# Block 1's norms in columns of tokens, the mix output's second half tile by tile, and the FFN's first weights split earlier

## The chip, the cores and the metric

The kernel runs on one core of one Trainium2 chip. The metric is device time in microseconds (us) of one execution; the times are given as the median of several runs, and the trace is of one profiled execution.

## The reference

Two blocks work on x of 512 tokens by 1024 features, in fp32. Block 1 has two layers; each is a norm, a projection with attention, a short convolution and gates (unchanged here), a projection of the merged branches back to 1024 features (the *mix output*), a second norm and an MLP with relu squared. Block 2 is one layer with a modulated norm, a token mixer and a SwiGLU FFN.

```python
def rmsnorm(x, g):
    xf = x.astype(jnp.float32)
    y = xf * lax.rsqrt(jnp.mean(xf * xf, axis=-1, keepdims=True) + EPS)
    return (y * g.astype(jnp.float32)).astype(x.dtype)
...
    for l in range(DEPTH):
        u = rmsnorm(x, norm_mix[l])
        proj = u @ w_in[l]
...
        x = x + merged @ w_mix_out[l]
        u = rmsnorm(x, norm_mlp[l])
        x = x + jnp.square(jax.nn.relu(u @ w_mlp_up[l])) @ w_mlp_down[l]
    return rmsnorm(x, norm_final)
...
        x = x + gt_m[:, None, :] * y
        h = modulate(rms_norm(x, g_ffn[l]), sh_f, sc_f)
        x = x + gt_f[:, None, :] * swiglu(h, w_gate[l], w_up[l], w_down[l])
```

## The kernel before

**Layout.** x stays in the chip's memory as eight tiles x0 to x7 of 128 features by 512 tokens. A weight matrix is streamed from DRAM in loads of 512 KB (`raw`, a ring of 8). Each load is split into a high part (`wh`, a cast on ScalarE, L217) and a low part (`wl`, a subtraction on VectorE, L218), and the activations are split likewise (`hilo`, L455 and L456; `prep`, L463 and L464, which also scales by the norm's gain). An fp32 product is then three matmuls (L279, L280, L281): high by high, high by low, low by high. A matmul on 512 columns of tokens fills one PSUM bank; four `mm` banks take the four output tiles that are under way.

**Order.** The program is a list of items. A *unit* is one piece of weights: at each unit the program issues the loads up to 5 units ahead and the splits up to 2 units ahead. *do* items run in their place; *bg* items are taken up one by one, so many to a unit as *rate* says. Each engine then works through its own queue in order, and semaphores hold an instruction until what it needs is there. So a matmul that waits holds every matmul behind it.

**Norm.** `square` adds up the squares of x0 to x7 in a tile `ss` (L494 on ScalarE, L495 on VectorE). `rstd` sums `ss` over the 128 partitions by a matmul with a matrix of ones (L501), and everything after it works on 128x512, although all partitions hold the same: a square root (L503), L504, a reciprocal (L505) and three steps of refinement (L511 to L513). The products with the weights don't wait for it, since they run on x times gain; the result `rs` enters as the banks are emptied (L928 for the MLP's first products).

**Mix output to MLP.** `linear` computes the mix output in two halves of four tiles; a half takes k-tiles 0 to 3 on all four tiles first and then k-tiles 4 to 7, in loads of 4 k-tiles by 256 columns. So x4 to x7 are finished 12 matmuls apart, at the very end (L912 adds the bank to x). The MLP's first 512 columns (`u0`) are a plain `linear`, in four pieces on the four banks; the other columns go by `seven`, seven products of half size in place of eight (L401 to L403, 256 columns each), for which sums and differences of x tiles are made (`mix`, L476 to L479, on tiles that L980 has scaled). These sums for four pairs of tiles (xk, xk+4) are background work during `u0`. `up(c)` and `down(c-1)` are then meshed.

**Norms in columns.** Block 1's end and block 2 already have another form: `colsum` (L1045) puts tokens on partitions (a 128x1 matmul for each 128 tokens), the arithmetic is done on 128x2 or 128x4, and `spread` (L1054, L1056) brings it back to all partitions by a diagonal matrix times ones. After layer 2's last `down`, the final norm and block 2's first norm run this way on each half of the tokens, then `hnorm` (L1066, L1076, L1079) writes block 2's input. Block 2's FFN starts the same way, with `gateup` (L1533 to L1535) as its first products and `y` (L1612) as scaling.

## Time and profile before

| | before |
|---|---|
| median of 3 runs | 2082.54 us (2080.67 to 2082.63) |
| profiled execution | 2082.21 us, span 2079.9 us |
| TensorE (PE) busy | 2041.5 us, 98% of the span |
| VectorE (DVE) busy | 1575.5 us, 76% |
| ScalarE (ACT) busy | 982.9 us, 47% |
| mean granted TensorE clock | 0.991 of full speed |

The span is the time from the first to the last instruction of the trace; 2.3 us of the profiled execution lie outside it. A matmul counts as busy whatever its clock. In the chain of work that ended last, PE has 91%.

### The profile page before, as it was taken

Reading aid. Unit: us, or ns where it says so; the run is one execution under the profiler, and the core shown is the slowest. Engines: PE = TensorE matmul, PEld = TensorE weight load, DVE = VectorE, ACT = ScalarE, POOL = GpSimd, SP = SyncE. Lnnn points to the kernel's source line nnn. Section 1 sums busy time; section 2 is a strip of 40 time slices with the busy share of each in tenths; the row PEclk is TensorE's granted clock in tenths of the full one; section 3 lists DMA queues with packets and bytes.
Section 4 is the critical chain, followed back from the end, with each engine's and each line's share of the span. In section 5 each row is a group of like instructions: output and inputs, shape, how many; then the busy total and the mean of one; then the engine's idle time right before and its main releaser. Section 6 shows DMA issues by size and latency. Waiting matters only on the chain.

```text
span 2079.9 us, 29624 instructions
## 1 busy us (share of the span) xinstructions
PE 2041.5 (98%) x11552; PEld 1759.0 (85%) x11552; DVE 1575.5 (76%) x2801; ACT 982.9 (47%) x1699; POOL 19.5 (1%) x33
## 2 busy tenths in 40 slices
PE   9999999899999999999998999999999998999999
PEld 7888888799999878888886999998877787999998
DVE  6999666797877669977667888877777378777775
ACT  5324773544444432339545444445477744443442
POOL 0000000000000000000000000000000000000000
PEclk9999999999999999999998999999999999999999
DMA  7333212244444333331223444443321112233331
GB/s 233 96 97 101 72 62 92 91 142 142 145 160 142 102 97 92 101 102 53 78 84 104 144 148 152 153 132 91 92 72 62 51 61 82 92 102 104 100 100 42
DMA packets 199020, 216.60 MB, mean 104 GB/s; under 512 B 10721, under 2 KB 178017, under 8 KB 198881
## 3 DMA queue, kind: packets, MB, share of 16 engines
q1 hardware_dynamic: 198880, 214.73, 32.8%
q8 instruction: 90, 1.47, 0.3%
q14 instruction: 50, 0.40, 0.1%
HBM read 212.60 MB, written 2.10 MB: 103 GB/s over the span
## 4 chain that ended last, share of the span: by engine, by line
PE 91%; DVE 6%; ACT 2%; issue 1%; DMA 0%; POOL 0%; SPq 0%; DVEq 0%; ACTq 0%; POOLq 0%
PE mm L279 13%; PE mm L280 13%; PE mm L281 13%; PE mm L401 7%; PE mm L402 7%; PE mm L403 7%; PE at L279 7%; PE at L280 7%; PE at L281 7%; PE at L540 1%; PE ot L574 1%; PE mm L430 1%; PE mm L431 1%; PE mm L432 1%; PE at L559 1%
## 5 line engine op out<-in xcount | busy, mean ns | idle before, releaser
L217 ACT CAST wh<-raw 128x1024 fp32r<-128x1024 f32 (+3 forms) x272 | 277.5, 1024 | 537.0 <-PE mm L280 220.1
L279 PE MATMUL mm<-g,wh 128*128 128x512 f32 (+2 forms) x1328 | 506.9, 383 | 2.4 <-ACT g L1076 1.6
L281 PE MATMUL mm<-g,wl 128*128 128x512 f32 (+2 forms) x1328 | 503.4, 379 | 0.0
L280 PE MATMUL mm<-g,wh 128*128 128x512 f32 (+2 forms) x1328 | 502.4, 379 | 0.0
L218 DVE TENSOR_TENSOR wl<-raw,wh 128x1024 fp32r<-128x1024 f32 (+3 forms) x272 | 321.6, 1184 | 128.5 <-ACT wh L217 127.2
L401 PE MATMUL mm<-g,wh 128*128 128x256 f32 x1288 | 367.7, 285 | 14.9 <-DVE g L928 12.6
L402 PE MATMUL mm<-g,wh 128*128 128x256 f32 x1288 | 367.4, 285 | 1.0 <-DVE g L456 1.0
L403 PE MATMUL mm<-g,wl 128*128 128x256 f32 x1288 | 367.3, 285 | 0.0
L279 PEld LDWEIGHTS mm<-g,wh 128*128 128x128 f32 (+1 forms) x1328 | 250.1, 189 | 51.8 <-issue 4.3
L280 PEld LDWEIGHTS mm<-g,wh 128*128 128x128 f32 (+1 forms) x1328 | 250.1, 188 | 45.7 <-issue 1.2
L281 PEld LDWEIGHTS mm<-g,wl 128*128 128x128 f32 (+1 forms) x1328 | 250.0, 188 | 45.7
L401 PEld LDWEIGHTS mm<-g,wh 128*128 128x128 f32 x1288 | 250.1, 194 | 22.4 <-issue 8.9
L402 PEld LDWEIGHTS mm<-g,wh 128*128 128x128 f32 x1288 | 249.6, 194 | 7.0 <-DVE g L456 1.4
L403 PEld LDWEIGHTS mm<-g,wl 128*128 128x128 f32 x1288 | 249.6, 194 | 0.5
L279 PE MATMUL at<-g,g 128*128 128x512 f32 x608 | 239.7, 394 | 1.4 <-ACT g L455 1.4
L280 PE MATMUL at<-g,g 128*128 128x512 f32 x608 | 239.5, 394 | 0.1
L281 PE MATMUL at<-g,g 128*128 128x512 f32 x608 | 237.7, 391 | 0.0
L217 ACT CAST wh<-ws 128x1024 fp32r<-128x1024 f32 x69 | 72.4, 1050 | 216.0 <-PE mm L402 205.2
L281 PEld LDWEIGHTS at<-g,g 128*128 128x128 f32 x608 | 114.7, 189 | 24.8
L279 PEld LDWEIGHTS at<-g,g 128*128 128x128 f32 x608 | 115.2, 189 | 22.4 <-ACT g L455 3.0
L280 PEld LDWEIGHTS at<-g,g 128*128 128x128 f32 x608 | 115.2, 190 | 19.5 <-DVE g L456 0.9
L218 DVE TENSOR_TENSOR wl<-ws,wh 128x1024 fp32r<-128x1024 f32 x69 | 84.4, 1223 | 60.6 <-ACT wh L217 60.6
(265 smaller groups left out, 2716.7 us busy)
## 6 DMA issues: line engine op xcount, KB each, us to landing
raw<-w_in SPq DMA_DIRECT2D x111, 512.0 KB, 3.8
raw<-w_mlp_up SPq DMA_DIRECT2D x64, 512.0 KB, 3.8
raw<-w_mlp_down SPq DMA_DIRECT2D x64, 512.0 KB, 3.4
g<-w_ada SPq DMA_DIRECT2D x96, 256.0 KB, 4.2
raw<-w_gate SPq DMA_DIRECT2D x22, 512.0 KB, 3.6
raw<-w_up SPq DMA_DIRECT2D x22, 512.0 KB, 3.6
raw<-w_down SPq DMA_DIRECT2D x22, 512.0 KB, 3.4
raw<-w_mix_out SPq DMA_DIRECT2D x16, 512.0 KB, 3.4
```

What stands on the lines that cost most here:

```text
L217: act.copy(hi, raw)
L218: dve.tensor_sub(lo, raw, hi.bitcast(F32))
L279: pe.matmul(ps, wh, hi[:, cs], start=st, stop=False)
L280: pe.matmul(ps, wh, lo[:, cs], start=False, stop=False)
L281: S["pe"] = pe.matmul(ps, wl, hi[:, cs], start=False, stop=en)
L401: pe.matmul(ps, wh, hi, start=first and m == 0 and k == 0, stop=False, skip_group_check=True)
L402: pe.matmul(ps, wh, lo, start=False, stop=False, skip_group_check=True)
L403: S["pe"] = pe.matmul(ps, wl, hi, start=False, stop=k == 3, skip_group_check=True)
L430: pe.matmul(ps, xh, wh, start=kb + k == 0, stop=False)
L431: pe.matmul(ps, xl, wh, start=False, stop=False)
L432: pe.matmul(ps, xh, wl, start=False, stop=kb + k == KT - 1)
L540: pe.matmul(ps[:, :WM], qs[hh][:, i * P : (i + 1) * P], ks[hh][n][:, :WM], start=n == 0, stop=n == 1)
```

## The change

1. **Norms.** The four norms inside block 1 go from `rstd` to `rstd1` (`colsum` into four columns, then arithmetic on 128x4) and `rstd2` (`spread` to 128x512 and a copy by ScalarE). `norm2` no longer collects the tokens' column with four instructions, since `rstd1` leaves it.
2. **Mix output.** Its second half is computed tile by tile: four units of 8 k-tiles by 128 columns, so that x4 to x7 are finished 24 matmuls apart. The operand sums `mix(0)` to `mix(2)` are issued right after x4, x5 and x6; `mix(3)` stays in the background of `u0`.
3. **mesh** puts each piece of `down` one piece of `up` later.
4. **Layer 2's end.** The last `up` is meshed with only the first half of `down(6)`; then come the first half of `down(7)` and, on two halves of the tokens, the second half of `down(6)` and `down(7)` in one.
5. **ahead.** From the second half of block 2's output projection until `gateup(1, 1)`, splits run up to 5 and loads up to 8 units ahead.

```diff
@@ -86,6 +86,8 @@
                 bg.extend(pay)
             elif kind == "rate":
                 rate = pay
+            elif kind == "ahead":
+                self.ahead, self.early = pay
             elif kind == "drain":
                 while bg:
                     bg.popleft()()
@@ -113,8 +115,11 @@
     out = []
     for i, x in enumerate(a):
         out.extend(x)
-        for p in b[i * len(b) // n : (i + 1) * len(b) // n]:
-            out.extend(p)
+        if i:
+            for p in b[(i - 1) * len(b) // n : i * len(b) // n]:
+                out.extend(p)
+    for p in b[(n - 1) * len(b) // n :]:
+        out.extend(p)
     return out
@@ -234,7 +239,7 @@
             us.append({"src": (ch, 0, ch[2], c, min(uw, ch[4] - c)), "narrow": narrow})
         return us
-    def linear(W, row0, kts, c0, widths, xs, evac, parts_=1, narrow=False, newbank=mmbank):
+    def linear(W, row0, kts, c0, widths, xs, evac, parts_=1, narrow=False, newbank=mmbank, bytile=False):
@@ -248,6 +253,10 @@
         TW = T // parts_
         steps = []
         kbase = 0
+        if bytile:
+            ch = chunk(W, row0, total, c0, cw)
+            steps = [(0, total, [{"src": (ch, 0, total, c, P)}]) for c in range(0, cw, P)]
+            kts = []
         for kt in kts:
             ch = chunk(W, row0 + kbase * P, kt, c0, cw)
             us = halves(ch, narrow)
@@ -494,17 +503,21 @@
             act.activation(sq[:, cs], x[j][:, cs], AF.Square, scale=scale)
             dve.tensor_add(S[key, "ss"][:, cs], S[key, "ss"][:, cs], sq[:, cs])
-    def rstd(key):
-
-        ps = atbank()
-        with tc.issue_after(S["pe"].ins):
-            pe.matmul(ps, ones, S[key, "ss"], start=True, stop=True)
-        sd, v, rs = slot(), slot(), slot()
-        act.activation(sd, ps, AF.Sqrt, bias=epsc, scale=1.0 / D)
-        dve.tensor_scalar(v, ps, 1.0 / D, EPS, op0=ALU.mult, op1=ALU.add)
-        dve.reciprocal(rs, sd)
-        refine(rs, v, sd)
-        S[key, "rs"] = rs
+    def rstd1(key):
+
+        ps, n = colsum([key], slice(0, T))
+        v, t, r = small(n, "m4"), small(n, "m4"), small(n, "rcol")
+        dve.tensor_scalar(v, ps[:, 0:n], EPS, None, op0=ALU.add)
+        act.activation(r, v, AF.Sqrt)
+        dve.reciprocal(r, r)
+        refine(r, v, t)
+        S["rcol"] = r
+
+    def rstd2(key):
+
+        ps = spread(S["rcol"], NT)
+        rs = S[key, "rs"] = slot()
+        act.copy(rs, ps)
     def refine(y, v, t):
@@ -703,24 +716,15 @@
                 nc.sync.dma_start(S[n], a["const"][:, o : o + T])
         def norm():
-            rstd("n")
+            rstd2("n")
             rs = S["n", "rs"]
             dve.tensor_mul(S["Cr"], S["Cr"], rs)
             dve.tensor_mul(S["Sr"], S["Sr"], rs)
         def norm2():
-            rs = S["n", "rs"]
             rs2 = slot()
-            dve.tensor_mul(rs2, rs, rs)
+            dve.tensor_mul(rs2, S["n", "rs"], S["n", "rs"])
             S["rs2"] = rs2
-            rcol = small(NT, "rcol")
-            for i in range(NT):
-                junk = small(P, "junk")
-                dve.scalar_tensor_tensor(
-                    junk, rs[:, i * P : (i + 1) * P], 1.0, ident,
-                    op0=ALU.mult, op1=ALU.mult, accum_out=rcol[:, i : i + 1],
-                )
-            S["rcol"] = rcol
         cc, cv, ycv = {}, {}, {}
@@ -737,12 +741,20 @@
             do(lambda: [square("n", j) for j in range(KT)])
         else:
             do(rope_tables)
-            add(gC)
+            add(gC[:3])
+            do(lambda: rstd1("n"))
+            add(gC[3:6])
+            do(norm)
+            add(gC[6:])
         gA = linear(W, 0, [4, 4], 1536, [P, P, 68], xs, evA)
-        at = 1 if l else 3
-        add(gA[:at])
-        do(norm)
-        add(gA[at:])
+        if l == 0:
+            add(gA[:1])
+            do(lambda: rstd1("n"))
+            add(gA[1:3])
+            do(norm)
+            add(gA[3:])
+        else:
+            add(gA)
         do(norm2)
@@ -911,10 +923,18 @@
                 j = 4 * g + j
                 dve.tensor_add(x[j], ps, x[j])
                 prep("n", j, col(C_NMLP + 8 * l + j))
-            return f
+                if 4 <= j < KT - 1:
+                    for step in mix("n", j - 4, y):
+                        step()
+            return f
+
+        def y(j):
+            t = slot()
+            act.activation(t, x[j], AF.Copy, scale=col(C_NMLP + 8 * l + j))
+            return t
         for g in range(2):
-            add(linear(a["w_mix_out"][l], 0, [4, 4], 512 * g, [P] * 4, lambda k: m[k], evmix(g)))
+            add(linear(a["w_mix_out"][l], 0, [4, 4], 512 * g, [P] * 4, lambda k: m[k], evmix(g), bytile=g == 1))
         do(m.clear)
@@ -954,18 +974,19 @@
         def up(c):
             return seven([(W_up, 512 * c), (W_up, 512 * c + 256)], xs, lambda k: S["n", "ta", k], lambda k: S["n", "tb", k], evup(c))
-        def down(c):
+        def down(c, gs=(0, 1), n=1, last=False):
+
             p = []
-            last = c == NU - 1
-            for g in range(2):
-                p += linear(a["w_mlp_down"][l], 512 * c, [4], 512 * g, [P] * 4, lambda k: hid[4 * c + k], evdn(c, g),
-                            parts_=2 if l == 1 and last and g == 1 else 1, narrow=not last, newbank=mmbank if last else atbank)
+            for g in gs:
+                p += linear(a["w_mlp_down"][l], 512 * c, [4] * n, 512 * g, [P] * 4, lambda k: hid[4 * c + k], evdn(c + n - 1, g),
+                            parts_=n, narrow=not last, newbank=mmbank if last else atbank)
             def free():
-                for k in range(4):
-                    hid.pop(4 * c + k)
-
-            p.append([("do", free)])
+                for k in range(4 * c, 4 * (c + n)):
+                    hid.pop(k)
+
+            if gs[-1]:
+                p.append([("do", free)])
             return p
         def freen():
@@ -975,29 +996,32 @@
                 S.pop(("n", "ta", k))
                 S.pop(("n", "tb", k))
-        def y(j):
-            t = slot()
-            act.activation(t, x[j], AF.Copy, scale=col(C_NMLP + 8 * l + j))
-            return t
-
         u0 = linear(W_up, 0, [4, 4], 0, [P] * 4, xs, ev0)
-        add(u0[:2])
-        do(lambda: rstd("n"))
-        I.append(("rate", 2.5))
-        I.append(("bg", [f for k in range(4) for f in mix("n", k, y)]))
-        add(u0[2:])
+        add(u0[:1])
+        do(lambda: rstd1("n"))
+        I.append(("bg", mix("n", 3, y)))
+        add(u0[1:3])
+        do(lambda: rstd2("n"))
+        add(u0[3:])
         I.append(("drain", None))
         do(ada_start)
         I.append(("rate", 0.25))
         I.append(("bg", [ada(n) for n in range(24 * l, 24 * l + 24)] + ([ada_end] if l else [])))
         for c in range(1, NU):
-            I.extend(mesh(up(c), down(c - 1)))
+            if l == 1 and c == NU - 1:
+                I.extend(mesh(up(c), down(c - 1, (0,))))
+            else:
+                I.extend(mesh(up(c), down(c - 1)))
         do(freen)
         I.append(("drain", None))
         do(ada_stop)
         if l == 1:
             do(sqrt_table)
-        add(down(NU - 1))
+            add(down(NU - 1, (0,), last=True))
+
+            add(down(NU - 2, (1,), 2, last=True))
+        else:
+            add(down(NU - 1, last=True))
     modp = cp.tile([P, 2, 48], F32, name="modp")
@@ -1495,6 +1519,8 @@
             p = linear(a["w_out_2"], 0, [4, 4], 512 * g, [P] * 4, mx, evout(g), parts_=1 + g)
             if g == 0:
                 p[2] = p[2] + [("do", mtail3)]
+            else:
+                I.append(("ahead", (5, 8)))
             add(p)
         do(O.clear)
         do(hm.clear)
@@ -1618,6 +1644,7 @@
         add(u0[8:])
         I.append(("rate", 2.0))
         I.append(("bg", [f for k in range(4) for f in mix("h", k, y)]))
+        I.append(("ahead", (2, 5)))
         add(gateup(1, 1))
         I.append(("drain", None))
         for c in range(2, NG - 1, 2):
```

**TensorE, layer 1, around the MLP norm's sum.** `mm` are banks, `g_713` to `g_725` the scaled tiles x0 to x3, `wh`/`wl` the split weights, `at_761` the bank of the norm. Before, the ones matmul L501 stands behind the 24 matmuls of `u0`'s first two pieces, into `mm_759` and `mm_760`:

```order
L279 MATMUL mm_760_3362<-g_724_3178,wh_738_3251 128x512
L280 MATMUL mm_760_3362<-g_725_3179,wh_738_3251 128x512
L281 MATMUL mm_760_3362<-g_724_3178,wl_739_3252 128x512
L501 MATMUL at_761_3375<-g_60_329,kon_89 128x512
L279 MATMUL mm_776_3410<-g_713_3114,wh_748_3299 128x512
L280 MATMUL mm_776_3410<-g_714_3115,wh_748_3299 128x512
L281 MATMUL mm_776_3410<-g_713_3114,wl_749_3300 128x512
```

After, with `at_783` for the sum, `ss` now called `g_713`, and `at_801` for the spread:

```order
L290 MATMUL mm_787_3434<-g_723_3182,wl_758_3306 128x512
L288 MATMUL mm_799_3471<-g_711_3117,wh_773_3364 128x512
L1069 MATMUL at_783_3420<-rdc_92,g_713_3121 128x1 x4
L289 MATMUL mm_799_3471<-g_712_3118,wh_773_3364 128x512
L290 MATMUL mm_799_3471<-g_711_3117,wl_774_3365 128x512
...
L288 MATMUL mm_782_3407<-g_730_3221,wh_780_3403 128x512
L289 MATMUL mm_782_3407<-g_731_3222,wh_780_3403 128x512
L1080 MATMUL at_801_3489<-g_800_3484,kon_89 128x512
L290 MATMUL mm_782_3407<-g_730_3221,wl_781_3404 128x512
L288 MATMUL mm_782_3407<-g_745_3278,wh_780_3403 128x512
```

The sum stands behind 25 matmuls of `u0`, those into `mm_782` and `mm_787` and one more; the spread follows 25 matmuls later, among the first products on x4 to x7.

**VectorE, same place.** Before, the reciprocal of 128x512 and the operand sums of all four pairs stand ahead of L928, which empties the first bank of `u0`:

```order
L504 TENSOR_SCALAR g_763_3378<-at_761_3375 128x512
L505 RECIPROCAL g_764_3379<-g_762_3377 128x512
L476 TENSOR_TENSOR g_770_3396<-g_768_3392 128x256
...
L218 TENSOR_TENSOR wl_841_3695<-raw_826_3616,wh_840_3694 128x1024
L476 TENSOR_TENSOR g_791_3464<-g_789_3460 128x256
L478 TENSOR_TENSOR g_791_3464<-g_789_3460,g_790_3462 128x256
L477 TENSOR_TENSOR g_792_3465<-g_790_3462,g_791_3464 128x256
L928 SCALAR_TENSOR_TENSOR g_793_3482<-mm_759_3349,g_764_3379 128x512
L479 TENSOR_TENSOR g_792_3465<-g_790_3462,g_792_3465 128x256
L456 TENSOR_TENSOR g_795_3486<-g_793_3482,g_794_3485 128x512
```

After, the sums of a pair stand behind the tile that completes it, and the small arithmetic ahead of the spread:

```order
L924 TENSOR_TENSOR x7_102<-mm_775_3368,x7_102 128x512
L486 TENSOR_TENSOR g_766_3347<-g_764_3344,g_765_3346 128x256
L487 TENSOR_TENSOR g_765_3346<-g_763_3342,g_764_3344 128x256
L488 TENSOR_TENSOR g_766_3347<-g_764_3344,g_766_3347 128x256
...
L512 RECIPROCAL rcol_786_3427<-rcol_786_3427 128x4
L524 TENSOR_TENSOR m4_785_3426<-rcol_786_3427 128x4
L525 SCALAR_TENSOR_TENSOR m4_785_3426<-m4_784_3425,m4_785_3426 128x4
L526 SCALAR_TENSOR_TENSOR rcol_786_3427<-m4_785_3426,rcol_786_3427 128x4
...
L1078 TENSOR_SCALAR g_800_3484<-kon_89,rcol_786_3427 128x128 x4
L223 TENSOR_TENSOR wl_814_3551<-ws_806_3510,wh_813_3550 128x1024
L339 TENSOR_TENSOR ws_806_3510<-ws_806_3510,raw_771_3360 128x1024
L948 SCALAR_TENSOR_TENSOR g_807_3524<-mm_782_3407,g_802_3491 128x512
```

L505 on 128x512 is gone; the twelve operand sums of the first three pairs have moved ahead of the last addition to `ss`; ahead of the first L948 (L928 before) stand the four parts of the diagonal (L1078) and two large instructions on weights.

**ScalarE, start of block 2's FFN.** L1076 (L1100 after) writes the normed operands of the second half of the tokens, L217 (L222 after) casts weights of `gateup`. Before:

```order
L1124 ACTIVATE n4_3321_16221<-n4_3322_16222 128x2
L1076 ACTIVATE g_3328_16239<-g_3326_16235,modc_91 128x256
L1076 ACTIVATE g_3331_16245<-g_3327_16237,modc_91 128x256
...
L1076 ACTIVATE g_3308_16094<-g_3340_16264,modc_91 128x256
L217 CAST g_3342_16275<-raw_3280_15955 128x512
L1076 ACTIVATE g_3310_16098<-g_3341_16268,modc_91 128x256
L217 CAST g_3346_16294<-raw_3280_15955 128x512
L217 CAST g_3349_16311<-raw_3289_16023 128x512
```

After, `g_3281`, `g_3285`, `g_3290` and `g_3294`, the casts of the next units, stand ahead of the norm of this half:

```order
L222 CAST g_3281_16006<-raw_3268_15952 128x512
L222 CAST g_3285_16036<-raw_3273_15990 128x512
L222 CAST g_3290_16068<-raw_3273_15990 128x512
L503 ACTIVATE g_3292_16085<-x4_99 128x256
L503 ACTIVATE g_3293_16101<-x5_100 128x256
L222 CAST g_3294_16104<-raw_3274_15992 128x512
...
L1148 ACTIVATE n4_3325_16300<-n4_3326_16301 128x2
L1100 ACTIVATE g_3332_16318<-g_3330_16314,modc_91 128x256
...
L1100 ACTIVATE g_3312_16173<-g_3344_16343,modc_91 128x256
L222 CAST g_3347_16356<-raw_3274_15992 128x512
L1100 ACTIVATE g_3314_16177<-g_3345_16347,modc_91 128x256
L222 CAST g_3350_16373<-raw_3289_16066 128x512
```

Before, the cast that the third group of `gateup` needs stood behind seven of the eight writes of the norm; after, four groups' casts stand ahead of all eight.

## Rows read from the trace of the kernel before

**Rows 1.** TensorE's waits over the whole run: total us, times, longest us.

```profile
PE mm L401 <- DVE g L928: 12.6, 4, 4.1
```

**Rows 2.** Four stretches: length, busy us (instructions) by engine, granted clock, DMA share, GB/s.

```profile
370.00:412.00 42.00, 34.37 (x155) 28.19 (x154) 31.24 (x47) 23.61 (x35) 0.00 (x0) 0.88 0.23 76
1080.00:1130.00 50.00, 40.21 (x185) 33.29 (x184) 36.10 (x57) 28.14 (x41) 0.00 (x0) 0.86 0.20 63
1430.00:1460.00 30.00, 25.60 (x183) 24.35 (x182) 23.54 (x75) 17.39 (x42) 0.00 (x0) 0.89 0.23 69
1710.00:1770.00 60.00, 52.54 (x331) 46.88 (x331) 52.21 (x105) 28.11 (x55) 0.00 (x0) 0.94 0.23 71
```

**Rows 3.** Timeline of TensorE, layer 1, end of `u0`: start, us, instruction, [idle before <- releaser].

```profile
383.85 0.39 PE L279 MATMUL mm<-g,wh 128*128 128x512 f32 x1
...
388.38 0.39 PE L281 MATMUL mm<-g,wl 128*128 128x512 f32 x1
392.82 0.36 PE L401 MATMUL mm<-g,wh 128*128 128x256 f32 x1 [4.06 <-DVE g L928]
```

**Rows 4.** Timeline of VectorE in the same stretch, the reciprocal and the operand sums.

```profile
375.09 3.34 DVE L505 RECIPROCAL g<-g 128x512 f32<-128x512 f32 x1
...
384.91 0.42 DVE L476 TENSOR_TENSOR g<-g 128x256 f32<-128x256 f32 x1
385.25 0.42 DVE L478 TENSOR_TENSOR g<-g,g 128x256 f32<-128x256 f32 x1
...
386.38 1.22 DVE L218 TENSOR_TENSOR wl<-ws,wh 128x1024 fp32r<-128x1024 f32 x1
387.51 0.68 DVE L456 TENSOR_TENSOR g<-g,g 128x512 fp32r<-128x512 f32 x1
```

**Rows 5.** Timeline of VectorE, layer 1, the mix output's second half.

```profile
362.75 0.75 DVE L464 SCALAR_TENSOR_TENSOR g<-x,cols,g 128x512 fp32r<-128x512 f32 x1
363.42 0.68 DVE L495 TENSOR_TENSOR g<-g,g 128x512 f32<-128x512 f32 x1
364.02 0.68 DVE L912 TENSOR_TENSOR x<-mm,x 128x512 f32<-128x512 f32 x1
```

**Rows 6.** Timeline of VectorE, then of TensorE, layer 1's first norm.

```profile
29.55 5.47 DVE L495 TENSOR_TENSOR g<-g,g 128x512 f32<-128x512 f32 x7 [1.09 <-ACT g L494]
35.80 1.02 PE L501 MATMUL at<-g,kon 128*128 128x512 f32 x2
```

**Rows 7.** Timeline of TensorE, block 2's FFN: a column sum, then 256-column matmuls.

```profile
1717.95 0.61 PE L1045 MATMUL at<-rdc,g 128*128 128x1 f32 x4
1718.42 0.36 PE L1534 MATMUL mm<-g,g 128*128 128x256 f32 x1
1718.62 0.28 PE L1535 MATMUL mm<-g,g 128*128 128x256 f32 x1
...
1719.68 0.28 PE L1535 MATMUL mm<-g,g 128*128 128x256 f32 x1
...
1725.80 0.58 PE L1533 MATMUL mm<-g,g 128*128 128x256 f32 x1 [4.63 <-ACT g L217]
```

**Rows 8.** Timeline of TensorE, then of VectorE, end of block 1.

```profile
1448.41 1.19 PE L1056 MATMUL at<-g,kon 128*128 128x256 f32 x2 [1.89 <-DVE g L1054]
1445.97 0.16 DVE L1102 TENSOR_SCALAR n<-at 128x2 f32<-128x2 f32 x1 [2.86 <-PE at L1045]
...
1447.79 0.48 DVE L1054 TENSOR_SCALAR g<-kon,n 128x128 f32<-128x128 f32 x2
```

**Rows 9.** Timeline of SP's queue, then of VectorE, start of block 2's FFN.

```profile
1727.90 1.57 SPq L182 DMA_DIRECT2D raw<-w_up  x2
1733.82 1.23 DVE L327 TENSOR_TENSOR ws<-raw,raw 128x1024 f32<-128x1024 f32 x1 [4.14 <-DMA raw<-w_up]
```

**Rows 10.** DMA issues: queue, operation, count, KB each, median us from issue to landing.

```profile
raw<-w_mix_out SPq DMA_DIRECT2D x16, 512.0 KB, 3.4
```

## The prediction

> **What bounds the kernel now.** TensorE is busy for 98% of the span, so time can come only from its waits, from stretches at half clock, or from fewer matmuls. I first read TensorE's waits: the largest kind is that for L928, which empties the banks of `u0`: 12.6 us in four waits [rows 1]. The timeline shows where: at 388.38 TensorE issues the last matmul of `u0` and then stands for 4.06 us, because no bank is free [rows 3]. VectorE, which should empty it, is late: it has 3.34 us of reciprocal in its queue, then the operand sums and splits, all ahead of L928 [rows 4]. Next I read the windows around every place where waits lie close together [rows 2]. There the reader can see two losses in each: length less TensorE's busy time is the wait, and one less the granted clock, times the length, is what the lower clock (1.2 in place of 2.4 GHz for parts of the stretch) took while matmuls ran:
>
> - layer 1, mix output to MLP (370 to 412): 7.6 + 0.12 x 42 = 12.7 us
> - layer 2, the same (1080 to 1130): 9.8 + 0.14 x 50 = 16.8 us
> - end of block 1 (1430 to 1460): 4.4 + 0.11 x 30 = 7.7 us
> - start of block 2's FFN (1710 to 1770): 7.5 + 0.06 x 60 = 11.1 us
>
> These 48.3 us are what the change can reach; the other stretches have next to nothing to give. The sum below is made against the profiled execution's 2082.2 us, which lies 0.3 us under the median of the runs.
>
> **Prices.** A 512-column matmul costs (388.38 - 383.85) / 20 = 0.227 us of TensorE [rows 3], a 256-column one (1719.68 - 1718.62) / 9 = 0.118 us, and a column sum of two columns 1718.42 - 1717.95 = 0.47 us, so four columns 0.94 us [rows 7]. The spread is a product of the ones with 512 columns, like L501 that it replaces, and I set both equal. On VectorE, queued behind its like, a 512-wide addition costs 0.60 us and L464 0.67 us [rows 5], an operand sum of 256 0.34 us, a split of 1024 1.13 us [rows 4].
>
> **The change, part by part.**
>
> *Four norms in columns.* Each adds 0.94 us of column sum to TensorE, which nothing hides. In layer 2's first norm that is all: -0.9 us. In layer 1's first norm the sum also stands six matmuls earlier than L501 did, at 35.80 - 6 x 0.227 = 34.4, but `ss` is only complete at 29.55 + 5.47 = 35.02 [rows 6]; with the semaphore TensorE waits some 0.65 us, and every matmul behind it too: -1.6 us. The spread there comes 13 matmuls later, and nothing waits.
>
> *Layers' mix output to MLP.* The reciprocal now works on 128x4 and drops out of VectorE's queue as a large item, and 12 of the 16 operand sums move ahead into the mix output. Does VectorE keep up there? A tile takes 24 x 0.227 = 5.44 us of TensorE. VectorE's work for one: addition 0.60, L464 0.67, square 0.60, four sums 1.36, two splits of sums 1.20, one split of weights 1.13, together 5.56 us. It is level with TensorE, hardly behind, and its queue holds no more than that. The first point of decision is the column sum: after the last matmul of x7, VectorE has an addition, three sums, a weight split, two splits of sums, L464 and the last addition to `ss` to do, 0.60 + 1.02 + 1.13 + 1.20 + 0.67 + 0.60 = 5.2, with the hand-overs 5.4 us; TensorE has 25 matmuls until it needs `ss`, 5.66 us. The second is the spread, again 25 matmuls (5.66 us) after the sum: VectorE has three sums 1.02, a weight split 1.13, two splits 1.20, four small instructions at 0.2 and the diagonal, 2 x 0.48 [rows 8], some 5.3 us with the small ones. Both margins are about 0.3 us, so I put 0.5 us of new waits into each layer; the least is 0, the most is in the first rival. The banks themselves come free early: after the spread 47 matmuls of `u0` remain, 10.7 us, for a copy, two weight instructions and the first L948. Then the whole loss of the stretch is given back: layer 1 12.7 - 0.9 - 0.5 = +11.3, layer 2 16.8 - 0.9 - 0.5 = +15.4 us. Layer 2's stretch holds one wait more, for a copy by ScalarE behind the loading of another table; in the new order this copy stands ahead of the loading.
>
> *End of block 1.* Before, the second spread stood four matmuls behind its column sum and waited 1.89 us for a chain that takes VectorE 1447.79 + 0.48 - 1445.97 = 2.3 us [rows 8]. Now ten matmuls stand there, 0.7 us more cover: about 1.2 us remain; the first spread has fewer matmuls ahead than before but a less crowded VectorE, 0.4 us by my reckoning, and the wait for the first normed operand some 0.5. So 2.1 of 4.4 us remain, and +2.3 us come back. Of the 3.3 us of clock I take half, 1.65, between nothing and all, since half of the waiting remains. The 48 matmuls of the fused `down` on 512 columns become 96 on 256: 48 x (2 x 0.118 - 0.227) = 0.4 us lost. Together +3.5 us (bounds +1.9 and +5.2).
>
> *Start of block 2's FFN.* TensorE waited 4.63 us for a weight cast that stood behind the norm's writes on ScalarE [rows 7]. The casts now stand ahead, so 37 matmuls, 4.4 us, can run while the norm's chain runs. But behind that wait VectorE is the bound: it waits 4.14 us for a load of `w_up`, until 1733.82, the second of two issued from 1727.90 on for want of a free `raw` [rows 9], and from there it works without a break for 35 us. So only what VectorE gains counts: three splits of 512 columns less in that stretch, 1.8 us, and a load that leaves about 2.2 us sooner, as its slot in the ring is free sooner (an estimate from the order of the splits). That is +4.0 us; the least is 0, the most the wait and the clock together, 4.4 + 3.6 = 8.0.
>
> *mesh.* One piece later is no later wait: in the steady loops TensorE has none of note, and `hid` is there even earlier than needed. 0.
>
> Sum: 11.3 + 15.4 + 3.5 + 4.0 - 1.6 - 0.9 = 31.7, so **2082.2 - 31.7 = 2050.5 us**.
>
> **The rivals.**
>
> *VectorE becomes the bound of the tile phase.* If its instructions take their full durations, since each waits for ScalarE's half of the pair, a tile costs 0.69 + 0.75 + 0.68 + 4 x 0.42 + 2 x 0.68 + 1.22 = 6.4 us [rows 4, 5], 0.95 more than TensorE; over three tiles it falls 2.9 us behind, and the tail behind x7 takes 6.2 in place of 5.4. The column sum then waits 2.9 + 6.2 - 5.66 = 3.4 us, in the middle of `u0`, and the clock falls as before for about 5 us of loss: 8.4 in place of 0.5 us in each layer, 15.8 us less gain, 2066 us. For it: the margin of 0.3 us. Against: in the rows of before VectorE does queue such work at the shorter spacing.
>
> *The FFN's gain is swallowed.* VectorE's 35 us without a break end no sooner, because the loads come no sooner, and TensorE waits later what it didn't wait before: 0 in place of 4.0, and at block 1's end only the lower bound of 1.9: 2050.5 + 5.6 = 2056 us. For it: VectorE's busy time in that stretch, 52 of 60 us [rows 2].
>
> *The waits go, the clock doesn't come back.* The change would then not do what it can: new short waits, of some tenths to 1.2 us, might be enough to keep the half clock in the same stretches. That takes back 5.0 + 7.0 + 1.65 = 13.7 us: 2064 us. For it: at block 1's end no wait is over 1.9 us, and still the clock is 0.89 on average [rows 2, 8]. The Trainium skill ("TensorE: Matmul & The Clock Gate", the section on why this matters for your kernels) says that the engine falls to the lower clock after a whole window without work; by that rule short waits would cost no clock and block 1's end would get all of its 3.3 us back, 2049 us. The row of block 1's end, with many short waits and yet a lost clock, speaks against it, so my sum doesn't use it.
>
> *Slower: the loads in short rows.* The tile units load 128 columns, rows of 512 bytes where there were 1 KB. This trace has no 512 KB load of that form. With rows of 1 KB a load of the mix output lands after 3.4 us [rows 10]; if the number of rows counted alone it would be 6.8 us, a little over a tile's 5.44, and five units of lead hide most of that. Only from about 10 us for each of the eight loads on, 4.5 us late each, does it eat the 31.7 us and 4 more: 2087 us. I see nothing in the profile that makes a load three times as long.
>
> **How the numbers follow.** 0.2%, 4.2 us, is about what a measurement of this kernel can tell from no change. Chances: the forecast 0.56, with a range of its own from 2043 (every lower bound of loss: 11.8 + 15.9 + 5.2 + 8.0 - 1.9 = 39 us) to 2054; VectorE the bound 0.16; the FFN's gain swallowed 0.14; no clock back 0.07; the short rows in full 0.04 and in part, so that the result is within 0.2%, 0.03. All but the last two are faster by over 0.2%: 0.93, 0.03, 0.04. The range for 8 in 10 reaches from 2043 to 2064, which leaves out most of the first rival.
>
> **What the profile of the changed kernel would show.** Right: no wait for L948 between `u0` and the first `seven` in either layer, granted clock near 1.00 over both stretches, the column sums directly behind the matmul before them. Wrong: a wait of the column sum (L1069) or the spread (L1080) for VectorE of more than 1 us; a clock of 0.9 in those windows with no long wait; in the FFN TensorE waiting later for casts, with VectorE still busy to the same point behind the norm; in the mix output's second half a cast that waits for a DMA.

## The result

The changed kernel takes 2050.07 us (median of 4 runs, 2048.67 to 2052.77) against 2082.59 us before (median of 4): a ratio of 0.9846, 95% interval 0.9829 to 0.9864, so 1.4 to 1.7% faster. The forecast was 2050.5 us. In a later run on another occasion the same program took 2050.63 us, ratio 0.9847 (0.9832 to 0.9861).

The first part of the page of the changed kernel, busy us by engine:

```profile
PE 2032.1 (99%) x11632; PEld 1755.4 (86%) x11632; DVE 1556.3 (76%) x2795; ACT 982.0 (48%) x1701; POOL 19.5 (1%) x33
```

TensorE is busy 9.4 us less, although it has 80 instructions more. The granted clock fits this: its mean over the run rose from 0.991 to 0.998 of full speed, so fewer matmuls run at half clock. TensorE's waits over the whole run that come to 0.5 us or more, largest first (total, times, longest):

```profile
PE mm L1559 <- ACT g L1100: 2.6, 1, 2.6
PE mm L1559 <- ACT g L222: 2.4, 3, 1.3
PE at L572 <- DVE nm L556: 2.0, 3, 0.9
PE at L665 <- DVE g L662: 1.5, 1, 1.5
PE at L1080 <- DVE g L1078: 1.3, 2, 1.2
PE mm L1561 <- DVE g L223: 1.3, 2, 1.1
PE at L553 <- POOL g L613: 0.7, 1, 0.7
PE at L1069 <- DVE g L504: 0.5, 1, 0.5
```

The 12.6 us for L928 [rows 1] have no successor: L948, its line now, isn't in the list. What remains is in the FFN (L1559, L1561), in places that the change doesn't touch (L572, L665, L553), and small: 1.3 us for spreads (1.2 of it at the end of block 1), 0.5 us for the column sum of layer 1's first norm. The same four places again, in windows 10 to 30 us earlier, since the kernel is ahead there:

```profile
360.00:400.00 40.00, 40.00 (x205) 33.83 (x204) 31.62 (x54) 26.36 (x38) 0.00 (x0) 1.00 0.29 93
1060.00:1110.00 50.00, 50.00 (x269) 42.87 (x268) 41.52 (x73) 32.09 (x47) 0.00 (x0) 1.00 0.36 116
1400.00:1430.00 30.00, 28.66 (x232) 27.74 (x231) 25.68 (x74) 19.37 (x43) 0.00 (x0) 1.00 0.37 104
1680.00:1740.00 60.00, 53.54 (x331) 47.91 (x330) 51.70 (x103) 26.02 (x51) 0.00 (x0) 0.94 0.21 65
```

Against [rows 2]: in both layers' step from mix output to MLP TensorE is busy without a gap at full clock. At the end of block 1 it has 1.3 us of waits left and the full clock. In the FFN nothing is won: 53.5 us busy of 60 at a clock of 0.94, where it was 52.5 of 60 at 0.94.

Three instructions of attention and mixer, which the change leaves alone, serve as milestones. The first stands behind layer 1's first norm, the second behind that of layer 2, the third in block 2's mixer. Before, then after (start, us, instruction, [idle before]):

```profile
265.71 0.30 PE L559 MATMUL at<-kon,g 128*128 128x128 f32 x1 [0.87 <-DVE nm L543]
977.49 0.30 PE L559 MATMUL at<-kon,g 128*128 128x128 f32 x1 [0.89 <-DVE nm L543]
1525.47 0.39 PE L540 MATMUL at<-g,g 128*128 128x256 f32 x1 [0.75 <-POOL g L600]
```

```profile
266.94 0.30 PE L572 MATMUL at<-kon,g 128*128 128x128 f32 x1 [0.89 <-DVE nm L556]
967.56 0.30 PE L572 MATMUL at<-kon,g 128*128 128x128 f32 x1 [0.88 <-DVE nm L556]
1494.80 0.39 PE L553 MATMUL at<-g,g 128*128 128x256 f32 x1 [0.75 <-POOL g L613]
```

At the first the changed kernel is 1.2 us behind, at the second 9.9 ahead, at the third 30.7 ahead, and at the end of the span (2079.9 against 2048.8) 31.1. Traces of the same code differ by about 1 us in such a distance, once by 2, so tenths count for little. From the milestones follow the terms, which the section after the experiments sets beside the prediction.

VectorE and TensorE in layer 1's step, at the two points of decision:

```profile
372.05 0.69 DVE L504 TENSOR_TENSOR g<-g,g 128x512 f32<-128x512 f32 x1
378.12 0.87 DVE L1078 TENSOR_SCALAR g<-kon,rcol 128x128 f32<-128x128 f32 x4
383.00 0.69 DVE L948 SCALAR_TENSOR_TENSOR g<-mm,g 128x512 f32<-128x512 f32 x1 [0.35 <-PE mm L290]
372.91 1.00 PE L1069 MATMUL at<-rdc,g 128*128 128x1 f32 x8
379.57 1.02 PE L1080 MATMUL at<-g,kon 128*128 128x512 f32 x2
```

The last addition to `ss` ends about 372.7 and the column sum starts at 372.91, right behind its predecessor; the diagonal ends at 378.99 and the spread starts at 379.57. These are margins of about 0.2 and 0.6 us, where the prediction had 0.25 and 0.35: VectorE comes just in time.

### The profile page after: what moved, and what is told of

Its sections match the earlier page's. It is cut to its first block, busy times and chain, and to the rows that moved or that the text cites. A ratio compares the mean times of both kernels' runs of the same rounds, so it can differ in the third digit from the quotient of the medians.

```text
span 2048.8 us, 29781 instructions
## 1 busy us (share of the span) xinstructions
PE 2032.1 (99%) x11632; PEld 1755.4 (86%) x11632; DVE 1556.3 (76%) x2795; ACT 982.0 (48%) x1701; POOL 19.5 (1%) x33
## 4 chain that ended last, share of the span: by engine, by line
PE 95%; DVE 3%; ACT 1%; issue 0%; DMA 0%; POOL 0%; SPq 0%; DVEq 0%; ACTq 0%; POOLq 0%
PE mm L288 14%; PE mm L289 14%; PE mm L290 14%; PE mm L412 8%; PE mm L411 8%; PE mm L410 8%; PE at L288 7%; PE at L289 7%; PE at L290 7%; PE at L553 1%; PE mm L439 1%; PE mm L440 1%; PE mm L441 1%; PE ot L587 1%; PE at L572 1%
## 5 line engine op out<-in xcount | busy, mean ns | idle before, releaser
L222 ACT CAST wh<-raw 128x1024 fp32r<-128x1024 f32 (+3 forms) x274 | 279.4, 1023 | 535.4 <-PE mm L411 224.0
L288 PE MATMUL mm<-g,wh 128*128 128x512 f32 (+1 forms) x1360 | 513.6, 379 | 0.4 <-ACT wh L222 0.3
L290 PE MATMUL mm<-g,wl 128*128 128x512 f32 (+1 forms) x1360 | 513.0, 377 | 0.0
L289 PE MATMUL mm<-g,wh 128*128 128x512 f32 (+1 forms) x1360 | 511.5, 376 | 0.0
L223 DVE TENSOR_TENSOR wl<-raw,wh 128x1024 fp32r<-128x1024 f32 (+3 forms) x274 | 324.2, 1185 | 145.3 <-ACT wh L222 144.3
L288 PEld LDWEIGHTS mm<-g,wh 128*128 128x128 f32 x1360 | 255.3, 188 | 49.6 <-issue 4.0
L290 PEld LDWEIGHTS mm<-g,wl 128*128 128x128 f32 x1360 | 255.4, 188 | 46.2 <-issue 1.0
L289 PEld LDWEIGHTS mm<-g,wh 128*128 128x128 f32 x1360 | 255.4, 188 | 45.3 <-issue 0.5
L410 PEld LDWEIGHTS mm<-g,wh 128*128 128x128 f32 x1288 | 246.8, 192 | 4.8 <-ACT g L1567 0.2
L411 PEld LDWEIGHTS mm<-g,wh 128*128 128x128 f32 x1288 | 246.8, 192 | 4.6
L412 PEld LDWEIGHTS mm<-g,wl 128*128 128x128 f32 x1288 | 246.8, 192 | 0.2
L288 PE MATMUL at<-g,g 128*128 128x512 f32 x592 | 231.8, 392 | 0.0
L289 PE MATMUL at<-g,g 128*128 128x512 f32 x592 | 231.8, 391 | 0.0
L290 PE MATMUL at<-g,g 128*128 128x512 f32 x592 | 230.4, 389 | 0.0
L222 ACT CAST wh<-ws 128x1024 fp32r<-128x1024 f32 x69 | 72.3, 1047 | 180.5 <-PE mm L411 170.1
L290 PEld LDWEIGHTS at<-g,g 128*128 128x128 f32 x592 | 111.2, 188 | 24.4 <-DVE g L223 0.5
L288 PEld LDWEIGHTS at<-g,g 128*128 128x128 f32 x592 | 111.6, 189 | 19.8
L289 PEld LDWEIGHTS at<-g,g 128*128 128x128 f32 x592 | 111.6, 189 | 18.6
L223 DVE TENSOR_TENSOR wl<-ws,wh 128x1024 fp32r<-128x1024 f32 x69 | 84.4, 1224 | 54.4 <-ACT wh L222 54.4
```

The lines of the kernel that those rows point to most:

```text
L222: act.copy(hi, raw)
L223: dve.tensor_sub(lo, raw, hi.bitcast(F32))
L288: pe.matmul(ps, wh, hi[:, cs], start=st, stop=False)
L289: pe.matmul(ps, wh, lo[:, cs], start=False, stop=False)
L290: S["pe"] = pe.matmul(ps, wl, hi[:, cs], start=False, stop=en)
L410: pe.matmul(ps, wh, hi, start=first and m == 0 and k == 0, stop=False, skip_group_check=True)
```

## The experiments

Each starts from the changed kernel, 2050.1 us, unless said otherwise. The kernel before was run beside each group of four: 2082.9 to 2083.3 us.

**Without the tiles.** Part 2 undone:

```diff
-                if 4 <= j < KT - 1:
-                    for step in mix("n", j - 4, y):
-                        step()
...
-            add(linear(..., evmix(g), bytile=g == 1))
+            add(linear(..., evmix(g)))
...
-        I.append(("bg", mix("n", 3, y)))
+        I.append(("rate", 2.5))
+        I.append(("bg", [f for k in range(4) for f in mix("n", k, y)]))
```

> The changed kernel (2050.1 us) with its part 2 undone: the mix output's second half in loads of 256 columns as before, all 16 operand sums in the background of u0 at rate 2.5; norms in columns, end of block 1 and early splits stay. Theory both: the columns take L504, the 3.34 us reciprocal and the refinement, 5.7 us together, out of VectorE's queue ahead of the first bank of u0, the tiles take 12 sums and their splits out of it; without the tiles the waits for L948 come back in part, 3 to 7 us with the clock in each layer: 2056 to 2064. Rival columns alone: the reciprocal was the whole reason, and the time stays at 2050 within 1. Rival tiles alone: the columns give nothing here, and nearly all of the 24 us that the two stretches gave back is lost again: about 2074.

Measured: 2071.55 us (2071.04 to 2073.18), ratio to before 0.9947 (0.9931 to 0.9964). TensorE's waits in layer 1's step:

```profile
PE mm L410 <- DVE g L945: 3.0, 1, 3.0
PE mm L410 <- ACT g L464: 2.2, 1, 2.2
PE mm L411 <- DVE g L465: 0.7, 1, 0.7
```

21.5 us are lost, so neither the range of theory "both" nor "columns alone" holds; it is close to "tiles alone" (2074). The reader sees the old pattern: a bank that isn't emptied (L945, the L948 of this kernel) for 3.0 instead of 4.1 us, then operands that come late. Layer 2 has the same three waits. The milestones of this kernel:

```profile
267.25 0.30 PE L572 MATMUL at<-kon,g 128*128 128x128 f32 x1 [0.89 <-DVE nm L556]
977.84 0.30 PE L572 MATMUL at<-kon,g 128*128 128x128 f32 x1 [0.88 <-DVE nm L556]
1514.71 0.39 PE L553 MATMUL at<-g,g 128*128 128x256 f32 x1 [0.75 <-POOL g L613]
```

From the first to the second it takes 710.6 us (before 711.8, the changed kernel 700.6), from the second to the third 536.9 (before 548.0, the changed kernel 527.2). So columns alone, with the sums in `u0`, give little in layer 1 but much in layer 2: with the 0.8 us that the column sum of layer 2's first norm costs added back, 2.0 us in layer 1; with the 4.2 us of block 1's end (below) taken off, 6.9 us in layer 2. Of these 6.9, 2.3 us are a wait of the kernel before that only layer 2 has, for a copy by ScalarE, and that is gone here:

```profile
PE mm L401 <- ACT g L354: 2.3, 1, 2.3
```

**Without the columns.** Part 1 undone: all four norms by `rstd` on 128x512 at their old places (TensorE again multiplies `ss` by the ones), `norm2` with its four instructions. In the MLP:

```diff
-        add(u0[:1])
-        do(lambda: rstd1("n"))
+        add(u0[:2])
+        do(lambda: rstd("n"))
         I.append(("bg", mix("n", 3, y)))
-        add(u0[1:3])
-        do(lambda: rstd2("n"))
-        add(u0[3:])
+        add(u0[2:])
```

> The changed kernel with its part 1 undone: all four norms inside block 1 on 128x512 again, at their places of before (in the MLP behind the first two pieces of u0); the second half of the mix output tile by tile, with the operand sums between, stays. It drops 4 x 0.94 us of column sums and the 0.5 us wait of layer 1's first norm from TensorE, 4.3 us. Theory both: VectorE has 5.7 us more to do ahead of L948, the waits for the banks come back in part, 3 to 7 us with the clock in each layer: 2052 to 2060. Rival tiles alone: 72 matmuls, 16 us, stand between the sum and the first product that needs a bank, which covers the wide norm too, and the kernel is faster than the changed one: 2046. Rival columns alone: the time goes back towards before, over 2070.

Measured: 2057.77 us (2056.89 to 2059.14), ratio 0.9879 (0.9864 to 0.9894): theory "both". Where it is lost:

```profile
PE at L290 <- DVE g L223: 2.3, 1, 2.3
PE at L288 <- ACT g L222: 1.5, 1, 1.5
```

No bank is waited for any more: the 72 matmuls do cover the wide norm, as the rival had it. But VectorE, with 5.7 us of wide norm in its queue where the columns need 1.9, is late with the things behind it, the splits of the first weights of `down`: 3.9 us in each layer with the casts, and the clock with it (0.86 over 10 us behind these waits in layer 1). The milestones of this kernel:

```profile
265.69 0.30 PE L584 MATMUL at<-kon,g 128*128 128x128 f32 x1 [0.88 <-DVE nm L568]
970.09 0.30 PE L584 MATMUL at<-kon,g 128*128 128x128 f32 x1 [0.87 <-DVE nm L568]
1503.51 0.39 PE L565 MATMUL at<-g,g 128*128 128x256 f32 x1 [0.75 <-POOL g L625]
```

Against the changed kernel it is 1.3 us ahead at the first, 2.5 behind at the second and 8.7 behind at the third. With 0.8 us saved in layer 2's first norm, the MLP's columns are worth 2.5 + 1.3 + 0.8 = 4.6 us in layer 1 and some 6 in layer 2, behind the place where I had looked for them, while in the first norms they only cost. The total hides two effects of opposite sign; the run with wide first norms, below, parts them. Read against the kernel before, the same milestones say what the tiles with the early sums give without any columns: 7.4 us in layer 1 and, less the 4.2 us of block 1's end, 10.4 in layer 2.

**Tiles, but the sums late.** Part 2 kept as to the weights, its operand sums moved back into the background of `u0` (the first and the last piece of the first diff above):

> The changed kernel with its second half of the mix output tile by tile, but the operand sums of all four pairs left in the background of u0 at rate 2.5, as before. Theory sums: the place of the sums is what freed VectorE ahead of L948; with them back in u0 the waits of the run without tiles (3.0, 2.2 and 0.7 us in each layer, with the clock 10 us) come back: 2066 to 2072. Rival spacing: it is the later, evener end of x4 to x7 that did it, and the sums find room: 2050 to 2054.

Measured: 2070.99 us (2070.03 to 2074.50), ratio 0.9947 (0.9932 to 0.9962).

```profile
PE mm L410 <- ACT g L464: 3.1, 1, 3.1
PE mm L410 <- DVE g L945: 3.0, 1, 3.0
```

The same time as without the tiles, and in layer 1 nearly the same waits: the even spacing of x4 to x7 by itself gives nothing, and it is the place of the sums that frees VectorE. That the spacing is needed to make room for them isn't shown: no run has early sums without the tiles.

**Without the early splits.** Part 5 undone, the two `ahead` lines:

> The changed kernel with its part 5 undone: splits 2 and loads 5 units ahead throughout. The traces of before and of the changed kernel put the gain of this part at 0.5 us instead of my 4.0, since TensorE now waits 2.6 us for L1100 and 2.4 us for splits later in the same stretch. Theory VectorE is the bound there: the time is 2050.5 within 1, the waits stand again at one place in front of the third group of gateup (4.6 us) and the clock is 0.94 over the stretch as with the change. Rival, my prediction's term: the part is worth 4 us and something else in this stretch took 3.5 us: 2054.

Measured: 2054.77 us (2053.04 to 2059.01), ratio 0.9867 (0.9852 to 0.9882), 4.7 us slower; its trace is 3.7 us longer. My theory of that moment, that the part is worth next to nothing because VectorE is the bound, falls; the prediction's term of 4 us stands. So does the larger part of its reason, that a load leaves about 2.2 us sooner. VectorE waits for that load of `w_up` first in this kernel, then in the changed one:

```profile
1703.41 1.23 DVE L336 TENSOR_TENSOR ws<-raw,raw 128x1024 f32<-128x1024 f32 x1 [4.29 <-DMA raw<-w_up]
```

```profile
1701.13 1.23 DVE L336 TENSOR_TENSOR ws<-raw,raw 128x1024 f32<-128x1024 f32 x1 [2.02 <-DMA raw<-w_up]
```

It goes on 2.3 us sooner. Then something else in the change must have taken about as much as the part gives in the same stretch.

**The old end of block 1.** Part 4 undone:

```diff
-            if l == 1 and c == NU - 1:
-                I.extend(mesh(up(c), down(c - 1, (0,))))
-            else:
-                I.extend(mesh(up(c), down(c - 1)))
+            I.extend(mesh(up(c), down(c - 1)))
...
             add(down(NU - 1, (0,), last=True))
-            add(down(NU - 2, (1,), 2, last=True))
+            add(down(NU - 1, (1,), 1, last=True, halves=2))
```

> The changed kernel with its part 4 undone: after layer 2's last up both halves of down(6) meshed, then down(7) with its second half on two halves of the tokens. By my prediction's term the part is worth 3.5 us: 2053.6. Theory the clock comes back in full: 5.0 us, the clock at the end of block 1 back to about 0.89 and the second spread waiting 1.9 us: 2055. Rival the part is worth nothing beside the column norms: 2050 within 1.

Measured: 2054.30 us (2053.04 to 2057.15), ratio 0.9864 (0.9849 to 0.9878), 4.2 us slower. The waits at this place:

```profile
1410.91 0.70 PE L1076 MATMUL at<-g,kon 128*128 128x256 f32 x2 [0.91 <-DVE g L1074]
1413.21 0.73 PE L288 MATMUL mm<-g,wh 128*128 128x256 f32 x4 [1.60 <-ACT g L1096]
1422.17 1.19 PE L1076 MATMUL at<-g,kon 128*128 128x256 f32 x2 [1.89 <-DVE g L1074]
```

These are the waits of before to the hundredth (0.91, 1.60 and 1.89 us; the last in [rows 8]); with the change one of 1.2 and one of 0.2 us are left. By this run the part is worth 4.2 us, between the two numbers expected. The clock isn't that of before, though. Over the 30 us around the same waits:

```profile
1400.00:1430.00 30.00, 25.60 (x193) 24.25 (x192) 25.52 (x79) 16.78 (x42) 0.00 (x0) 0.94 0.30 86
```

0.94 where it was 0.89 [rows 2]: the same waits cost 1.8 us of clock here and 3.3 us in the kernel before.

**Block 2's mesh as before.** What else differs in the FFN? Of the traces, the kernel without early splits waits at the end of the busy stretch a third time, which the kernel before doesn't. The only part of the change that reaches there is the shift in `mesh`. Undone in block 2 alone, with the old function as `mesh0`:

```diff
-            I.extend(mesh(unit(c) + unit(c + 1), down(c // 2 - 1)))
-        I.extend(mesh(unit(NG - 1), down(ND - 2)))
+            I.extend(mesh0(unit(c) + unit(c + 1), down(c // 2 - 1)))
+        I.extend(mesh0(unit(NG - 1), down(ND - 2)))
```

> The changed kernel with part 3, the later pieces of down, undone in block 2 alone (a piece of down stands in the mesh where it stood before; block 1 keeps the shift). Theory: the early splits gave back the 4 us that the prediction's term said, and the shifted mesh took 3.2 us of them, since at the end of the FFN's busy stretch TensorE now waits 1.3 and 1.1 us for casts and splits, and the clock falls to 0.66 for 5 us behind, where before a piece of down stood there and the clock stayed up: 2050.1 less 3.2, 2047. Rival mesh costs nothing, as predicted, and the stretch differs by the order of loads: 2050 within 1.

Measured: 2049.11 us (2048.81 to 2050.30), ratio 0.9839 (0.9824 to 0.9853). The end of the busy stretch in the changed kernel, and then in this one:

```profile
1734.45 0.50 PE L1559 MATMUL mm<-g,g 128*128 128x512 f32 x1 [1.31 <-ACT g L222]
1736.39 0.76 PE L1561 MATMUL mm<-g,g 128*128 128x512 f32 x1 [1.06 <-DVE g L223]
```

```profile
1735.60 0.50 PE L1570 MATMUL mm<-g,g 128*128 128x512 f32 x1 [1.34 <-ACT g L233]
```

The wait of 1.06 us is gone, and the granted clock of the last 20 us of the stretch is 1.00:

```profile
1724.00:1744.00 20.00, 17.62 (x74) 13.93 (x73) 15.81 (x28) 6.65 (x12) 0.00 (x0) 0.91 0.18 56
```

```profile
1726.00:1746.00 20.00, 18.66 (x99) 15.46 (x98) 16.76 (x29) 8.62 (x15) 0.00 (x0) 1.00 0.18 53
```

From the third milestone (1496.60 here) to the end of the trace (2047.3) this kernel gains 3.3 us on the changed one. But in the times only 1.0 to 1.5 us show, and the intervals of the two ratios overlap: the wait is there, its price isn't settled by this run.

What makes the wait is not a piece of `down` that is missing on TensorE, as I had expected. TensorE's order around it is the same in both kernels, and the first piece of `down` comes only behind it, at 1751.61 in the changed kernel and at 1747.16 here. The order differs on VectorE. The changed kernel, then this one:

```profile
1734.52 1.22 DVE L336 TENSOR_TENSOR ws<-raw,raw 128x1024 f32<-128x1024 f32 x1
1735.65 0.68 DVE L223 TENSOR_TENSOR g<-raw,g 128x512 fp32r<-128x512 f32 x1
```

```profile
1735.67 0.68 DVE L234 TENSOR_TENSOR g<-raw,g 128x512 fp32r<-128x512 f32 x1
...
1741.00 1.22 DVE L347 TENSOR_TENSOR ws<-raw,raw 128x1024 f32<-128x1024 f32 x1
```

L336 (L347 here) adds up weights for the first `seven` product; in the changed kernel it stands ahead of the split L223 that TensorE waits for, and without the shift behind it. It takes VectorE 1.1 us, about the length of the wait. The run without early splits, the changed kernel run again and the next run have the sum ahead of the split as well, the kernel before and that of wide first norms have it behind. By which step the shifted list brings the sum forward isn't shown.

**The shift in block 2 alone, on the kernel before.** The same two lines the other way round, nothing else of the change:

> The kernel before with one part of the change alone: in block 2's mesh each piece of down stands one piece later; nothing else. Theory: this is what took the FFN's gain, so it makes the kernel before slower by about 3.3 us, 2086, with one more wait of about 1 us at the end of the FFN's busy stretch and half clock behind it. Rival, the prediction's 0: 2082.6 to 2083.3, unchanged.

Measured: 2084.75 us (10 runs, 2083.43 to 2086.51), ratio 1.0008 (0.9998 to 1.0018).

```profile
1765.49 0.50 PE L1547 MATMUL mm<-g,g 128*128 128x512 f32 x1 [0.73 <-ACT g L231]
1770.19 0.50 PE L1547 MATMUL mm<-g,g 128*128 128x512 f32 x1 [1.33 <-ACT g L231]
1772.13 0.50 PE L1549 MATMUL mm<-g,g 128*128 128x512 f32 x1 [1.06 <-DVE g L232]
```

The first two waits, 0.73 and 1.33 us, are in the kernel before too; the third, 1.06 us, is new, as expected. The clock stayed at 1.00 this time, so the rest of the 3.3 us didn't come. The times alone can't tell this kernel from the one before, since the interval of the ratio includes 1; the wait is in the trace. The shift thus brings 1.1 us of waiting, and up to 2 more where the clock falls behind it.

**Block 1's mesh as before.** The same two calls in block 1:

> The changed kernel with part 3 undone in block 1 alone. Theory: in block 1 the shift is needed, because the first piece of down stands behind the first seven and needs the high and low parts of hid that ScalarE and VectorE write behind L948; without it TensorE waits 1.5 to 3 us there in each layer, with some clock: 2053 to 2058. Rival, the prediction's 0 for the mesh: 2050 within 1.

Measured: 2050.79 us (2049.76 to 2051.54), ratio 0.9845 (0.9831 to 0.9860): unchanged, and both stretches (360 to 405, 1070 to 1110) still have TensorE busy without a gap. The rival holds; block 1 doesn't need the shift.

**Wide first norms.** The kernel with block 2's mesh as before, now with the layers' first norms on 128x512 at their old places, the MLP norms in columns:

> The kernel of the run before last (block 2's mesh as before) with the two first norms of block 1's layers on 128x512 again, at their places of before; the two MLP norms stay in columns. Theory: columns cost TensorE 0.94 us in each first norm and 0.5 us of waiting in layer 1's, and bring nothing there, since nothing on VectorE is late at these places: 2.4 us less than that run, 2044.5 if it comes to 2047. Rival: VectorE's longer chain shows as a wait of the first products that need the norm, and the time is that of that run within 1.

Measured: 2044.88 us (2044.61 to 2045.46), ratio 0.9818 (0.9801 to 0.9834), 4.2 us less than with block 2's mesh alone and 5.2 us less than the changed kernel: the fastest of this study. That is more than the 2.4 us expected, but the excess lies in the kernel that it is measured by. The third milestone, here and in the kernel with block 2's mesh as before:

```profile
1492.81 0.38 PE L576 MATMUL at<-g,g 128*128 128x256 f32 x1 [0.75 <-POOL g L636]
```

```profile
1496.60 0.39 PE L564 MATMUL at<-g,g 128*128 128x256 f32 x1 [0.74 <-POOL g L624]
```

These are 3.8 us. But up to there that kernel has the code of the changed one, whose two traces reach the place at 1494.80 and 1495.18; against these, wide first norms gain 2.0 and 2.4 us, as expected. The rival is refuted.

**GpSimd for eight additions.** In that kernel, `dve.tensor_add` in block 2's `y` becomes `nc.gpsimd.tensor_add`:

> The kernel of the run before (e7) with the eight additions of 512 columns that rebuild the scaled tiles for the operand sums of block 2's FFN (y, 4.8 us of VectorE in the busy stretch) done by GpSimd. Theory VectorE is the bound of this stretch: the last waits of the stretch (1.3 and 1.1 us) go and it is 2 to 4 us faster than e7. Rival: GpSimd is slower at it than VectorE or holds VectorE up, and the sums come later: as e7 or slower.

Measured: 2048.03 us (2047.65 to 2048.36), ratio 0.9832 (0.9818 to 0.9847), 3.1 us slower. One addition takes GpSimd 1.74 us on average, against 0.60 for one of many in a row on VectorE [rows 5]:

```profile
L1662 POOL TENSOR_TENSOR g<-g,g 128x512 f32<-128x512 f32 x8 | 13.7, 1739 | 144.6 <-PE mm L1585 130.4 <-DVE g L1127 14.2
```

The last wait of the stretch shrinks from 1.3 to 0.3 us, but earlier in the FFN's start waits of 1.9 and 1.3 us for operands of `gateup` and of 1.1 us for a split stand instead. The rival's time holds; why these operands come later isn't shown.

**Splits 8 ahead.** `("ahead", (5, 8))` becomes `("ahead", (8, 12))` in the fastest kernel:

> The fastest kernel so far (e7, 2044.9 us: block 2's mesh as before, the layers' first norms on 128x512) with splits 8 and loads 12 units ahead, in place of 5 and 8, from the second half of block 2's output projection to gateup(1, 1). Theory: the three waits for casts (0.7, 0.4 and 0.2 us) that stand behind the norm's writes in the FFN go, and up to 2 us with the clock behind: 2043 to 2044. Rival: VectorE stays the bound, later waits take the place of these: 2045 within 1.

Measured: 2046.32 us (2045.98 to 2046.60), ratio 0.9826 (0.9811 to 0.9840), 1.4 us slower. It lies outside both ranges, but the rival's mechanism is there. The three waits for casts go, and later waits take their place: a column sum waits 1.4 us for an addition of squares (L515), and `gateup` 2.1 us for a bank that ScalarE empties late (L1591).

**The changed kernel again.**

> The changed kernel unaltered, on the same chip as the other runs of this call, to say how far its waits and its time repeat: 2050 within 1, waits of 2.6, 1.3 and 1.1 us in the FFN.

Measured: 2050.63 us (2050.06 to 2051.58). The waits of 1.3 and 1.1 us at the end of the FFN's stretch repeat; the one of 2.6 us is 1.5 here.

## Why the prediction was right, point by point

The total was right, 2050.5 against 2050.07 us. Its terms, in us, from the milestones and the runs:

| term | forecast | measured |
|---|---|---|
| layer 1's first norm | -1.6 | -1.2 |
| layer 2's first norm | -0.9 | -0.8 (0.81 from the column sum's start to the next matmul's; no wait) |
| mix output to MLP, layer 1 | +11.3 | +12.0 (9.93 + 1.23 + 0.81) |
| layer 2's step and block 1's end | 15.4 + 3.5 = +18.9 | +20.7 (30.67 - 9.93) |
| of these, block 1's end | +3.5 | +4.2 (part 4 undone) |
| FFN, early splits | +4.0 | +4.7, 3.7 by the trace (part 5 undone) |
| FFN, mesh | 0 | -1.0 to -3.3 (block 2's part 3 undone), about -3 by nine traces |
| FFN together | +4.0 | +0.4 (31.1 - 30.7) |

*The steps to the MLP* were right in place and size, with no new wait where I had set 0.5 us aside in each layer. The rival that VectorE becomes the bound is refuted for this kernel by margins of 0.2 and 0.6 us, not by much: 3.8 us more of VectorE's work (5.7 in place of 1.9) cost 3.9 us of waits in the run without columns. What the prediction put together as one cause the experiments part. By the milestones, less the first norm and block 1's end, the two steps gave back, in us:

| | layer 1 | layer 2 |
|---|---|---|
| columns alone (run without the tiles) | 2.0 | 6.9 |
| tiles with early sums alone (run without the columns) | 7.4 | 10.4 |
| both (changed kernel) | 12.0 | 16.5 |

The early sums are the larger part, some 10 us in each layer beside the columns; the columns are worth some 5 beside the early sums, and by themselves 2 and 7. The two nearly add up. The numbers of layer 2 are less 4.2 us for block 1's end; by the clock that the kernel before lost there, 1.5 us more than the run of the old end, each would be 1.5 us lower.

*Layer 1's first norm* waits 0.50 us for `ss`, expected 0.65, and a column sum of four columns costs 0.8 to 0.9 us where the prediction had 0.94. *Block 1's end* gave more, since 3.1 us of waits came back in place of 2.3, and the clock whole, not half: it is 1.00 in that stretch, and the waits of 1.2 and 0.2 us that were left cost no clock there. The rule of the Trainium skill that the prediction weighed ("TensorE: Matmul & The Clock Gate", the section on why this matters for your kernels) says that TensorE falls to the lower clock after a whole window without work. It fits what is left at this place better than my forecast did. It fits neither this place before, where waits of at most 1.89 us went with a clock of 0.89, nor the end of the FFN's stretch, where the clock falls to 0.91 over 20 us behind waits of 1.3 and 1.1 us.

*The rival that the clock doesn't come back* is refuted: 1.00 in three of the four stretches.

*The FFN* is the step that failed: "mesh. One piece later is no later wait ... 0". I had looked for a `down` that comes too late for its own operands, and only at the steady loops. What the shift changed is VectorE's order ahead of the first loop: a sum of weights came to stand in front of a split that TensorE needs, which makes a wait of 1.06 us, and in most traces the clock falls behind it. The rival "the FFN's gain is swallowed" thus came true for the FFN's own sum, with another cause than the loads. Its price follows from the distance between the third milestone and the end of the trace, in us:

| | without the shift in block 2 | with it |
|---|---|---|
| splits as before | 554.4 (before) | 555.9 (shift alone), 557.6 (without early splits) |
| early splits | 550.7, 550.0 (block 2's mesh as before, wide first norms) | 552.2 to 554.4, mean 553.4 (seven traces) |

The early splits give 3.7 to 4.4 us without the shift, and the shift takes back about 3 of them. The seven traces are the changed kernel, its repetition and the runs without tiles, without columns, with late sums, with the old end of block 1 and with block 1's mesh as before; they share the code of this stretch. The loss was made up for by 3 us more than forecast in the terms ahead of it, so the total being right to half a us is in part luck.

*The loads in short rows*: no wait of an engine for a mix output's load shows in any trace.

What stays open: how much of the FFN's sum is the clock, and why. In the changed kernel's trace it falls to 0.91 in two stretches of 20 us, in the run of the shift alone such waits cost no clock, and the wait for L1100 differs by 1.1 us between two traces of one program.

## What to carry to other kernels

When an engine off the critical path is late at one place, look for what can be moved ahead of that place into a stretch where it has room, before making its instructions cheaper: here the moved sums were worth some 10 us a layer, the norm's cheaper arithmetic some 5 beside them. A change of form pays only where somebody waits: the same column norm cost 1 us each at the two places where nobody did, and leaving it out there, with block 2's mesh as before, gave the fastest kernel, 2044.9 us. And price a reordering at every place and on every engine that it reaches, not only at the one that it was made for: the shift of `down` left TensorE's order at the late wait as it was, and moved a sum of weights on VectorE in front of the split that TensorE needed.
